# Later due times for side steps of a two-layer hybrid kernel: scan units split in three, and norm, filter, turn and gate steps placed behind more projections

## The chip, the cores and the metric

The kernel runs on one core of one Trainium2 chip, in one launch. The metric is the device time of an execution in microseconds (us). The same kernel varies from run to run by about 0.2%, so two medians that differ by less than that are not told apart.

## The reference

Two layers work on 128 context tokens and 512 latent tokens of width 1024. Each layer has a token mixer of three branches and then a SwiGLU FFN; both have a norm, a modulation and a gated residual. Cut to what the change touches:

```python
def trunk_layer(x, mod, s0, p):
    sh1, sc1, g1, sh2, sc2, g2 = jnp.split(mod, 6, axis=-1)
    h = rmsnorm(x, p['norm1_g']) * (1.0 + sc1) + sh1
    y, s_fin = parallel_mixer(h, s0, p)
    x = x + g1 * y
    h = rmsnorm(x, p['norm2_g']) * (1.0 + sc2) + sh2
    x = x + g2 * swiglu(h, p['w_gu'], p['w_down'])
...
def delta_mixer(qkv_raw, z, b_raw, a_raw, conv_w, a_log, dt_bias, norm_w, s0):
    qkv = jax.nn.silu(centred_dwconv(qkv_raw, conv_w).astype(f32))
    q = l2norm(qkv[..., :H_A * DK].reshape(bn, L, H_A, DK)) * (DK ** -0.5)
    k = l2norm(qkv[..., H_A * DK:2 * H_A * DK].reshape(bn, L, H_A, DK))
    beta = jax.nn.sigmoid(b_raw.astype(f32))
    g = -jnp.exp(a_log.astype(f32)) * jax.nn.softplus(a_raw.astype(f32) + dt_bias.astype(f32))
    # forward and backward gated_delta_chunked(q, k, v, g, beta, s0)
...
def gated_delta_chunked(q, k, v, g, beta, s0):      # chunks of 64 tokens
    decay = jnp.exp(jnp.where(incl, gc[..., :, None] - gc[..., None, :], -jnp.inf))
    a_low = jnp.where(strict, jnp.einsum('bhnid,bhnjd->bhnij', kb, k) * decay, 0.0)
    m = a_low + jnp.eye(CHUNK, dtype=a_low.dtype)
    u = triangular_solve(m, v * beta[..., None])     # and w; then a scan over chunks
...
def hyena_filters(L, w1, b1, freq, w2, b2, w3):
    h = jnp.sin(fq * (zpos @ w1.astype(f32) + b1.astype(f32)))
    h = jnp.sin(fq * (h @ w2.astype(f32) + b2.astype(f32)))
    h = h @ w3.astype(f32)                           # then a window, and an FFT over tokens
```

## The kernel before

All 640 tokens are worked on together as two halves of 320 columns (`c` = 0, 1), channels on partitions. A projection is a sum of products of 128x128 weights with 128x320 activations. Each fp32 product is made of three matmuls of split operands (`wh`, `wl` are the upper and lower part of a weight tile). Three such matmuls, `pg<-A,wh` twice and `pg<-A,wl` once, are called a *triple* below.

The order of the instructions on all engines is fixed when the program is written out, and it is a planner that fixes it. There is a main stream, the projections of a layer in turn (q, k, v; FNet input; z; Hyena input; gates; output; FFN). Beside it run *side* coroutines, which hold the work that isn't a projection: `filters` (the Hyena filter network and its transform), `delta_gates`, `delta_qk` (normalises q and k and turns them), `delta_v`, the three batches of the chunked scan (`prep` with `delta_unit` and `delta_inv`, and `scan` with `delta_step`), `mods`, `fnet`, `hyena`, and `rstd` (the two halves of a norm's reciprocal root). After every two triples the main stream calls `pump`, which may let a side do its next step, up to its next `yield`. It does so when the time at which the step's inputs will be ready, as a crude cost model has it (`co.t`), is not later than the modelled time of TensorE:

```python
for co in sorted(self.sides, key=lambda co: co.t):
    ...
    if not co.done and self.ready(co) and co.t <= c["pe"] + co.hint:
        self.step(co)
```

So a number added to `cur.t` inside a side puts its next step further back among the projections. Where the main stream needs a side's result, it calls `finish`, and the steps that are left are written out in a row with no projection between them. There are three such places in a layer that matter here. One is behind the v projections of layer 1, `self.finish(self.ff, self.gm)`, where the rest of the filter network must be done. The next is ahead of the gates:

```python
while self.dst() is None:
    self.finish_one(gd)
```

`dst` is the end of batch 1, the four forward latent chunks of the scan. The third is the end of a norm, whose normalised tiles the next projections need.

A scan unit (`delta_unit`, 10 for a layer, four to a batch and two in batch 0) is a chunk pair in one direction. Before, its first step has three GpSimd passes of 128x512: two that make the right sides `rhs` from the gate sums `dgh` (written as `U<-dgh,small`), and one that makes mask times beta (`small,dsel`). The next step has the two matmuls `ps<-U,stcr` on the right sides, an exponential on ScalarE, and a GpSimd product. `stagger` runs two units side by side. `delta_inv` then inverts the 64x64 systems (matmuls `A,A 32x32` are its first stage), and `delta_step` runs the scan (`S,A` are its products with the state).

Every operation goes through one helper line, L2189, so all instructions of the trace have that line; they are told apart by tiles. `T`, `U`, `A` are pools of work tiles of 640, 512 and 2560 columns, `ps` and `pg` are tiles of PSUM, `rb` the broadcast reciprocal root. `stcr`, `par`, `small` are constants, `dgh`, `dsel`, `dex` results of `delta_gates`, `dsr` and `dss` of the rsqrt in `delta_qk`.

Of the kernel before, what the change touches and what calls it, by code (L numbers as in the profile page):

```python
# [303 lines left out]
class _Net:  # L304
# [472 lines left out]
    def rstd(self, u, n, w):  # L777

        nc = self.nc
        if u == 0:  # L780
            self.rb = []
        self.on(self.ssq[:, u:u + n * w])
        yield 0.0
        ps = self.ps()
        for t in range(n):
            nc.tensor.matmul(ps[:w, t:t + 1], self.ssq[:, u + t * w:u + t * w + w], self.ones[:, 0:1],
                             start=True, stop=True)
        m = self.p2.tile([P, 5], F32, tag="nm", name=self.nm("nm"))[:w, :n]
        r = self.p2.tile([P, 5], F32, tag="nr", name=self.nm("nr"))[:w, :n]
        nc.vector.tensor_scalar(out=m, in0=ps[:w, :n], scalar1=1.0 / D, scalar2=EPS, op0=ALU.mult, op1=ALU.add)  # L790
        self.rsqrt(r, m)
        dg = (self.U() if u or n * w < T else self.Tt())[:w, :n * w]
        nc.vector.tensor_tensor(out=dg.rearrange("p (t j) -> p t j", t=n),
                                in0=self.ident[:w, None, :w].to_broadcast([w, n, w]),
                                in1=r[:, :, None].to_broadcast([w, n, w]), op=ALU.mult)
        yield 0.0
        for c in range(n * w // NC):
            ps = self.ps()
            nc.tensor.matmul(ps[:, :NC], self.ones[:w], dg[:, c * NC:(c + 1) * NC], start=True, stop=True)
            self.rb.append(ps[:, :NC])  # L800
# [117 lines left out]
    def filters(self, l):  # L918
# [30 lines left out]
        for sl in (slice(0, TS), slice(TS, T)):  # L949
            n = sl.stop - sl.start  # L950
            ps = self.ps()
            nc.tensor.matmul(ps[:64, :n], mw[:33, 0:64], zp[:33, sl], start=True, stop=True)
            self.sin_mlp(ps[:64, :n], 64, fq[:64], bb[:64, 0:1], h1[:64, sl], n)
            yield
            ps = self.ps()
            nc.tensor.matmul(ps[:, :n], mw[:64, 64:192], h1[:64, sl], start=True, stop=True)
            h2 = self.U()
            self.sin_mlp(ps[:, :n], P, fq, bb[:, 1:2], h2[:, :n], n)
            nc.scalar.copy(hs[:64, sl], h2[:64, :n])
            th = self.U(F32R)  # L960
            nc.scalar.copy(th[64:, :n], h2[64:, :n])
            nc.vector.tensor_tensor(out=hs[64:, sl], in0=h2[64:, :n], in1=th[64:, :n].bitcast(F32), op=ALU.subtract)
            yield
        if not l:
            self.pre = True
# [144 lines left out]
    def delta_qk(self):  # L1110

        nc = self.nc
        self.kt = self.A()
        kt = self.kt.rearrange("p (t c) -> p t c", t=5)
        q, k = self.q, self.k
        def one(t):
            cols = slice(t * P, (t + 1) * P)
            ss = self.p2.tile([P, 16], F32, tag="dss", name=self.nm("dss"), bufs=3)
            qn = self.U()
            for n, (src, dst) in enumerate(((q, qn), (k, kt[:, t]))):  # L1120
                ps = self.ps()
                for m in range(4):
                    nc.tensor.transpose(ps[:, m * P:(m + 1) * P], src[:, m, cols], self.ident)
                sq = self.U()
                nc.scalar.activation(sq, ps, AF.Square)
                nc.scalar.copy(dst, ps)
                nc.vector.tensor_reduce(out=ss[:, n * 8:n * 8 + 8], in_=sq.rearrange("p (h d) -> p h d", d=64),
                                        axis=AX.X, op=ALU.add)
            yield
            r = self.p2.tile([P, 16], F32, tag="dsr", name=self.nm("dsr"), bufs=3)  # L1130
            nc.vector.tensor_scalar(out=ss, in0=ss, scalar1=EPS, scalar2=None, op0=ALU.add)
            self.rsqrt(r, ss)
            nc.vector.tensor_scalar(out=r[:, 0:8], in0=r[:, 0:8], scalar1=0.125, scalar2=None, op0=ALU.mult)
            for n, dst in enumerate((qn, kt[:, t])):
                dv = dst.rearrange("p (h d) -> p h d", d=64)
                nc.vector.tensor_tensor(out=dv, in0=dv, in1=r[:, n * 8:n * 8 + 8, None].to_broadcast([P, 8, 64]),
                                        op=ALU.mult)
            yield
            for src, dst in ((qn, q), (kt[:, t], k)):
                ps = self.ps()  # L1140
                for m in range(4):
                    nc.tensor.transpose(ps[:, m * P:(m + 1) * P], src[:, m * P:(m + 1) * P], self.ident)
                nc.scalar.copy(dst[:, :, cols], ps.rearrange("p (m t) -> p m t", m=4))

        yield from self.stagger([one(t) for t in range(5)], 3)

    def delta_v(self):
# [12 lines left out]
    def delta_gates(self, l, ba):  # L1160
# [2 lines left out]
        nc = self.nc  # L1163
        v = nc.vector
        ab = self.par[l][1]
        ps = self.ps()
        for t in range(5):
            nc.tensor.transpose(ps[:, t * 32:(t + 1) * 32], ba[:32, t * P:(t + 1) * P], self.ident[:32, :32])
# [62 lines left out]
    def delta_unit(self, N, Pm, u, s, t):  # L1231

        nc = self.nc
        rhs = []
        mk = self.mask[:, s]
        for n in range(2):
            r = self.U(F32R)
            nc.gpsimd.tensor_tensor(out=r.rearrange("p (c i) -> p c i", i=64),
                                    in0=self.ghl[:, n, s, t, :, None].bitcast(F32).to_broadcast([P, 8, 64]),
                                    in1=mk[:, None, :].to_broadcast([P, 8, 64]), op=ALU.mult)  # L1240
            rhs.append(r)
        E, mb = N[:, u], Pm[u]
        nc.gpsimd.tensor_tensor(out=mb, in0=mk[:, None, :].to_broadcast([P, 8, 64]),
                                in1=self.beta[:, s, t].rearrange("p b a -> p (b a)")[:, :, None].to_broadcast([P, 8, 64]),
                                op=ALU.mult)
        yield
        ps = self.ps()
        nc.tensor.matmul(ps, self.stcr[:, s], rhs[0], start=True, stop=False)
        nc.tensor.matmul(ps, self.stcr[:, s], rhs[1], start=False, stop=True)
        nc.scalar.activation(E, ps.rearrange("p (c i) -> p c i", i=64), AF.Exp)  # L1250
        nc.gpsimd.tensor_tensor(out=E, in0=E, in1=mb, op=ALU.mult)
        yield
        pk = [self.ps(), self.ps()]
        for hh in range(4):
            for n, src in enumerate((self.k, self.q)):
                for h2, par in DIAG:
                    pr = slice(64 * h2, 64 * h2 + 64)
                    c0 = t * P + par * 64
                    nc.tensor.matmul(pk[h2][64 * par:64 * par + 64, hh * P + n * 64:hh * P + n * 64 + 64],
                                     self.k[pr, hh, c0:c0 + 64], src[pr, hh, c0:c0 + 64], start=True, stop=True)  # L1260
        for h2 in range(2):
            pv = pk[h2].rearrange("p (c n i) -> p c n i", c=4, n=2)
            for dst, n in ((Pm[u], 1), (N[:, u], 0)):
                nc.vector.tensor_tensor(out=dst[:, h2 * 4:h2 * 4 + 4], in0=pv[:, :, n], in1=E[:, h2 * 4:h2 * 4 + 4],
                                        op=ALU.mult)
        yield
# [392 lines left out]
    def hyena(self, l):  # L1659
# [3 lines left out]
        for hf in range(2):  # L1663
# [4 lines left out]
            nc.sync.dma_start(z[:, :, 0:TP], src[:, :, 0:TP])  # L1668
            nc.sync.dma_start(z[:, :, TP:T], src[:, :, TP + 1:T + 1])
            self.on(S)  # L1670
            yield
            for o in range(2):
                zs = z[:, :, TP:T]
# [566 lines left out]
```

## Time and profile before

| | us |
|---|---|
| runs | 2749.70, 2753.47, 2746.98 (median 2749.7) |
| profiled execution | 2748.93, of which the span of the trace is 2747.2 |
| TensorE (PE) busy | 2542.1 (93%) |
| VectorE (DVE) busy | 1784.8 (65%) |
| GpSimd (POOL) busy | 1272.3 (46%) |
| ScalarE (ACT) busy | 1101.5 (40%) |

TensorE's mean granted clock over the span was 0.963 of full speed. "Idle" in the text is time in which TensorE runs no matmul; the profile names the instruction that ended each such wait.

### The profile page before, as it was taken

What the parts mean: (1) busy time and instruction counts of PE and PEld (TensorE: products, weight loads), DVE (VectorE), ACT (ScalarE), POOL (GpSimd) and SP (SyncE); (2) the same over time, 40 slices, a digit from 0 to 9 for tenths busy, and PEclk for the clock granted to TensorE, in tenths of its full rate; (3) what the DMA queues carried; (4) which work ended last, traced back from release to release, by engine and by line L of the source; (5) the groups of instructions that cost most, each with busy time, mean ns of one, the idle gap of its engine ahead of it and who ended that gap; (6) DMA issues with size and microseconds to landing.
All of it is one profiled execution on the core that took longest, in us unless ns stands there. A gap on an engine that the chain in (4) does not pass through costs nothing. (4 is left out here: it accounts for less than half of the span.)

```text
span 2747.2 us, 55957 instructions
## 1 busy us (share of the span) xinstructions
PE 2542.1 (93%) x22520; PEld 2411.4 (88%) x22520; DVE 1784.8 (65%) x3375; ACT 1101.5 (40%) x2383; POOL 1272.3 (46%) x1228
## 2 busy tenths in 40 slices
PE   5897999979999999999988989889999999999998
PEld 3786988979999999999977779778889998999997
DVE  5467977444645686667665789665456358777775
ACT  4454464422332343333335544534223333444442
POOL 2334325332335576666632352333333365776662
PEclk8998999989999999999989999989999999999999
DMA  7442663534554235422222437425255441222222
GB/s 295 171 164 63 162 146 90 155 134 146 204 191 169 62 128 173 162 78 85 85 97 90 144 79 184 115 65 159 95 200 193 163 167 47 85 85 77 85 76 79
DMA packets 125683, 353.57 MB, mean 129 GB/s; under 512 B 11994, under 2 KB 26330, under 8 KB 118944
## 3 DMA queue, kind: packets, MB, share of 16 engines
q1 hardware_dynamic: 107856, 312.76, 34.2%
q0 software_dynamic: 17568, 37.24, 7.1%
q8 instruction: 177, 2.90, 0.4%
q14 instruction: 82, 0.67, 0.1%
HBM read 288.60 MB, written 37.24 MB: 119 GB/s over the span
## 5 line engine op out<-in xcount | busy, mean ns | idle before, releaser
L2189 PE MATMUL pg<-A,wh 128*128 128x320 f32 (+1 forms) x6304 | 1456.0, 318 | 44.3 <-POOL A L2189 10.4
L2189 PEld LDWEIGHTS pg<-A,wh 128*128 128x128 f32 (+1 forms) x6304 | 1070.5, 192 | 87.0 <-POOL A L2189 18.0
L2189 PE MATMUL pg<-A,wl 128*128 128x320 f32 (+1 forms) x3152 | 990.5, 314 | 2.3 <-DMA wl<-wr 1.8
L2189 POOL TENSOR_TENSOR wl<-wr,wh 128x512 fp32r<-128x512 f32 (+2 forms) x374 | 524.3, 1415 | 513.8 <-ACT wh L2189 486.4
L2189 PEld LDWEIGHTS pg<-A,wl 128*128 128x128 f32 (+1 forms) x3152 | 603.5, 191 | 7.1 <-DMA wl<-wr 4.2
L2189 ACT CAST wh<-wr 128x512 fp32r<-128x512 f32 (+2 forms) x486 | 287.0, 609 | 278.8 <-PE pg L2189 231.4
L2189 PE MATMUL ps<-A,wh 128*128 128x320 f32 x1696 | 378.8, 310 | 0.0
L2189 PEld LDWEIGHTS ps<-A,wh 128*128 128x128 f32 x1696 | 283.9, 188 | 1.4 <-issue 1.0
L2189 PE MATMUL ps<-A,wl 128*128 128x320 f32 x848 | 263.5, 311 | 5.0 <-POOL wl L2189 4.8
L2189 POOL TENSOR_TENSOR wl<-U,wh 128x512 fp32r<-128x512 f32 x160 | 227.8, 1441 | 43.5 <-ACT wh L2189 43.5
L2189 POOL DMA_DIRECT2D wl<-wr x112 | 98.7, 912 | 277.7 <-ACT wl L2189 264.6
L2189 PE MATMUL ps<-A,A 32*32 32x32 f32 (+5 forms) x2984 | 205.3, 239 | 9.3 <-DVE A L2189 5.5
L2189 PEld LDWEIGHTS ps<-A,A 32*32 32x32 f32 (+2 forms) x2984 | 177.3, 142 | 20.2 <-DVE A L2189 6.0
L2189 DVE TENSOR_TENSOR T<-T,T 128x320 f32<-128x320 f32 (+1 forms) x139 | 133.6, 961 | 83.7 <-ACT T L2189 79.4
L2189 POOL TENSOR_TENSOR A<-A,A 128x640 fp32r<-128x640 f32 (+5 forms) x84 | 122.2, 1473 | 121.0 <-ACT A L2189 113.1
L2189 DVE TENSOR_TENSOR A<-A 128x120 f32<-128x120 f32 (+23 forms) x690 | 161.0, 297 | 14.0 <-DMA A<-hyS 10.8
L2189 PEld LDWEIGHTS ps<-A,wl 128*128 128x128 f32 x848 | 159.7, 188 | 7.4 <-POOL wl L2189 7.3
L2189 ACT CAST wh<-U 128x512 fp32r<-128x512 f32 x160 | 99.2, 621 | 165.4 <-PE ps L2189 60.0
L2189 PE MATMUL pg<-A,A 128*128 128x320 f32 x1056 | 161.0, 310 | 0.0
L2189 PEld LDWEIGHTS pg<-A,A 128*128 128x128 f32 x1056 | 156.3, 188 | 0.7 <-issue 0.2
L2189 DVE STREAM_TRANSPOSE A<-A 32x1024 f32<-32x1024 f32 x72 | 151.2, 2120 | 1.5
L2189 DVE TENSOR_TENSOR U<-ps,U 128x512 f32<-128x512 f32 x144 | 77.9, 542 | 103.3 <-PE ps L2189 66.8
(165 smaller groups left out, 3194.7 us busy)
## 6 DMA issues: line engine op xcount, KB each, us to landing
wr<-in_wbig_dram SPq DMA_DIRECT2D x272, 512.0 KB, 3.7
A<-in_wmod_dram SPq DMA_DIRECT2D x40, 1024.0 KB, 6.4
A<-hT SPq DMA_DIRECT2D x32, 1024.0 KB, 7.7
wl<-wr POOLq DMA_DIRECT2D x112, 256.0 KB, 4.5
kSp<-U SPq DMA_DIRECT2D x40, 256.0 KB, 2.0
U<-kSp SPq DMA_DIRECT2D x40, 256.0 KB, 8.7
A<-in_wmod_dram SPq DMA_DIRECT2D x16, 512.0 KB, 10.2
hyS<-T SPq DMA_DIRECT2D x24, 320.5 KB, 3.1
```

The costliest lines, as they stand in the source:

```text
L2189: return f(*a, **k)
```

## The change

No instruction changes its operands. Numbers are added to the due times of some steps, and three `yield` lines are new: one at the start of `delta_gates`, with a wait on its input, and one behind each of the two `rhs` passes of `delta_unit`, so that the unit's three GpSimd passes stand in three steps.

```diff
     def rstd(self, u, n, w):            # u > 0: second half of a norm
         self.on(self.ssq[:, u:u + n * w])
+        if u:
+            self.cur.t += 3.0
         yield 0.0
...
+        if u:
+            self.cur.t += 3.0
         yield 0.0
         for c in range(n * w // NC):
...
     def filters(self, l):               # after the first, and after the second sin step
+            if l:
+                self.cur.t += 3.0
             yield
...
     def delta_qk(self):
+            self.cur.t += 2.0
             yield
             for src, dst in ((qn, q), (kt[:, t], k)):
...
     def delta_gates(self, l, ba):
         ab = self.par[l][1]
+        self.on(ba[:32])
+        self.cur.t += 2.5
+        yield
         ps = self.ps()
...
     def delta_unit(self, N, Pm, u, s, t):
             rhs.append(r)
+            self.cur.t += 1.5
+            yield
         E, mb = N[:, u], Pm[u]
...
     def hyena(self, l):
             self.on(S)
+            self.cur.t += 1.5
             yield
```

What this does to the order is seen best on TensorE, at three places.

The first is in layer 0, the two units of batch 0 (`U,stcr`) among the k and v projections. Before:

```order
L2189 MATMUL pg_2317<-A_449,wl_2119 128x320
L2189 MATMUL ps_2345<-U_2329,stcr 128x512
L2189 MATMUL ps_2345<-U_2331,stcr 128x512
L2189 MATMUL ps_2350<-U_2334,stcr 128x512
L2189 MATMUL ps_2350<-U_2336,stcr 128x512
L2189 MATMUL pg_2317<-A_450,wh_2123 128x320
```

And in the changed kernel, where the units come behind the rest of that projection and behind the start of the next one (`pg_2366`):

```order
L2204 MATMUL pg_2317<-A_450,wl_2124 128x320
L2204 MATMUL ps_2360<-small,A_428 128x128 x4
L2204 MATMUL pg_2366<-A_449,wh_2118 128x320
L2204 MATMUL pg_2366<-A_451,wh_2118 128x320
L2204 MATMUL pg_2366<-A_449,wl_2119 128x320
L2204 MATMUL pg_2366<-A_449,wh_2118 128x320
L2204 MATMUL pg_2366<-A_451,wh_2118 128x320
L2204 MATMUL pg_2366<-A_449,wl_2119 128x320
L2204 MATMUL ps_2373<-U_2329,stcr 128x512
L2204 MATMUL ps_2373<-U_2339,stcr 128x512
L2204 MATMUL ps_2378<-U_2331,stcr 128x512
L2204 MATMUL ps_2378<-U_2341,stcr 128x512
```

The four matmuls have moved behind six more triples. On GpSimd the passes of the two units stood as two `rhs`, one mask, two `rhs`, one mask; now the four `rhs` come first and the two masks last, still six in a row.

The second place is in layer 1, where the filter network (`U,T` its taps, `A,A` its transform) runs beside the last q, k, v projections. Before, pieces of it alternate with pairs of triples up to the end of the projections:

```order
L2189 MATMUL ps_17196<-U_17050,T_16221 128x512
L2189 MATMUL ps_17196<-U_17051,T_16221 128x512
L2189 MATMUL pg_17203<-A_15731,wh_16951 128x320
L2189 MATMUL pg_17203<-A_15733,wh_16951 128x320
L2189 MATMUL pg_17203<-A_15731,wl_16952 128x320
L2189 MATMUL pg_17203<-A_15731,wh_16951 128x320
L2189 MATMUL pg_17203<-A_15733,wh_16951 128x320
L2189 MATMUL pg_17203<-A_15731,wl_16952 128x320
L2189 MATMUL ps_17210<-A_16687,A_16685 128x512
L2189 MATMUL ps_17210<-A_16688,A_16685 128x512
L2189 MATMUL ps_17210<-A_16687,A_16685 128x512
```

At the same rows of the changed kernel the projections have run out, and filter work follows filter work:

```order
L2204 MATMUL pg_17061<-A_15732,wh_16868 128x320
L2204 MATMUL pg_17061<-A_15734,wh_16868 128x320
L2204 MATMUL pg_17061<-A_15732,wl_16869 128x320
L2204 MATMUL ps_17133<-U_16962,T_16221 128x512
L2204 MATMUL ps_17133<-U_16963,T_16221 128x512
L2204 MATMUL ps_17145<-U_16962,T_16221 128x512
L2204 MATMUL ps_17145<-U_16963,T_16221 128x512
L2204 MATMUL ps_17152<-A_16806,A_16804 128x512
L2204 MATMUL ps_17152<-A_16807,A_16804 128x512
```

Behind the last q, k, v projection there stand 10 `U,T` and 48 `A,A` matmuls before, and 26 and 84 now; 28 triples have moved ahead of that filter work. The steps of the filter network ahead of it, its sines and first taps, stand 4 to 26 triples later.

The third place is the end of layer 1's Hyena projections, ahead of the loop on `dst`. Before, units of the last batch still have projections beside them:

```order
L2189 MATMUL ps_20100<-A_17945 64x64 x16
L2189 MATMUL ps_20119<-U_20027,stcr 128x512
L2189 MATMUL ps_20119<-U_20029,stcr 128x512
L2189 MATMUL pg_20018<-A_15732,wh_19617 128x320
L2189 MATMUL pg_20018<-A_15734,wh_19617 128x320
L2189 MATMUL pg_20018<-A_15732,wl_19618 128x320
```

Now the last projections stand ahead of the first forward step of the scan, and nothing of the main stream is left behind them:

```order
L2204 MATMUL pg_19753<-A_15732,wh_19559 128x320
L2204 MATMUL pg_19753<-A_15734,wh_19559 128x320
L2204 MATMUL pg_19753<-A_15732,wl_19560 128x320
L2204 MATMUL ps_19882<-A_17804 64x64 x16
L2204 MATMUL ps_19906<-U_19899,U_19808 64x64
L2204 MATMUL ps_19907<-U_19899,U_19808 64x64 x2
```

Thirty triples that stood beside the scan have moved ahead of it. All four forward steps (`S,A`), the last 128 matmuls of the last batch's first inverse stage, and its units now lie behind the last projection; before, one step of four and the inverse stage lay ahead of it.

Elsewhere the moves are smaller, counted in triples on TensorE. The transposes of `delta_gates` move back by 8 (layer 0) and 12 (layer 1). The turns of `delta_qk` move by 2 to 4. The first products of a Hyena half move by 2 to 4. The second half of a norm moves too: the column sums (`small,T`) by 8, and then the broadcast (`U,small`), which stood 8 triples behind the sums of layer 1's FFN norm, stands behind 4 triples and 30 other matmuls of the same size. The broadcast of layer 1's first norm moves by 8 triples. The number of matmuls, and of instructions on VectorE and GpSimd, is the same.

## Rows read from the trace of the kernel before

**Rows 1.** Page: the span, and busy time, share and instructions of two engines

```profile
span 2747.2 us, 55957 instructions
PE 2542.1 (93%) x22520; PEld 2411.4 (88%) x22520; DVE 1784.8 (65%) x3375; ACT 1101.5 (40%) x2383; POOL 1272.3 (46%) x1228
```

**Rows 2.** Waits of TensorE: whom for, us in total, times, longest

```profile
PE ps L2189 <- POOL U L2189: 8.7, 11, 2.1
```

**Rows 3.** Timeline of TensorE, layer 0: start, us, operation [idle before, releaser]

```profile
94.28 0.61 PE L2189 MATMUL ps<-small,T 32*128 32x32 f32 x5 [2.30 <-DVE T L2189]
...
126.51 1.51 PE L2189 MATMUL ps<-U,T 128*128 128x512 f32 x2 [4.70 <-ACT U L2189]
...
211.96 0.63 PE L2189 MATMUL ps<-small,U 128*128 128x128 f32 x4 [3.25 <-DVE U L2189]
...
229.02 1.12 PE L2189 MATMUL ps<-small,A 128*128 128x128 f32 x4 [5.13 <-ACT A L2189]
...
243.95 0.50 PE L2189 MATMUL ps<-U,stcr 128*128 128x512 f32 x1 [2.13 <-POOL U L2189]
```

**Rows 4.** Timeline of TensorE, layer 1 up to q, k, v

```profile
1446.89 0.49 PE L2189 MATMUL ps<-small,T 32*128 32x32 f32 x5 [2.31 <-DVE T L2189]
...
1483.18 0.48 PE L2189 MATMUL ps<-T,U 64*128 64x128 f32 x2 [3.87 <-ACT T L2189]
...
1501.25 0.50 PE L2189 MATMUL ps<-U,T 128*128 128x512 f32 x1 [1.44 <-ACT U L2189]
...
1582.52 0.92 PE L2189 MATMUL ps<-small,U 128*128 128x128 f32 x4 [2.97 <-DVE U L2189]
```

**Rows 5.** Stretches: us, busy PE, PEld, DVE, ACT, POOL; PEclk, DMA share, GB/s

```profile
94.30:100.00 5.70, 5.70 (x51) 4.54 (x52) 2.56 (x8) 2.98 (x8) 0.00 (x0) 0.70 1.05 368
...
243.90:254.00 10.10, 8.16 (x62) 6.56 (x66) 6.55 (x2) 3.39 (x7) 5.41 (x6) 0.66 0.19 56
...
1447.00:1452.00 5.00, 5.00 (x23) 3.96 (x24) 2.21 (x7) 4.37 (x8) 0.00 (x0) 0.76 0.44 163
...
1483.20:1488.00 4.80, 4.35 (x19) 4.16 (x20) 2.02 (x2) 2.63 (x8) 2.66 (x6) 0.64 0.00 0
```

**Rows 6.** A stretch of layer 1's last q, k, v projections, columns as in rows 5

```profile
1526.00:1555.00 29.00, 29.00 (x148) 23.51 (x147) 19.03 (x27) 15.09 (x37) 10.26 (x17) 1.00 0.60 185
```

**Rows 7.** Layer 1, last q, k turn: TensorE, VectorE, GpSimd timelines

```profile
1602.64 1.09 PE L2189 MATMUL ps<-small,U 128*128 128x128 f32 x4 [6.41 <-DVE U L2189]
...
1594.57 0.18 DVE L2189 SCALAR_TENSOR_TENSOR rs<-rs,dss 128x16 f32<-128x16 f32 x1
1594.78 6.78 DVE L2189 SCALAR_TENSOR_TENSOR dsr<-rs,dsr 128x16 f32<-128x16 f32 x1
...
1595.18 2.37 POOL L2189 TENSOR_TENSOR U<-dgh,small 128x512 fp32r<-128x512 f32 x2
...
1600.19 1.33 POOL L2189 TENSOR_TENSOR U<-small,dsel 128x512 f32<-128x512 f32 x1
```

**Rows 8.** Layer 1, scan: TensorE timeline, and stretches as in rows 5

```profile
1756.05 3.12 PE L2189 MATMUL ps<-A,A 32*32 32x32 f32 x126 [3.93 <-DVE A L2189]
...
1788.49 1.97 PE L2189 MATMUL ps<-A 64*64 64x64 f32 x32 [8.06 <-DVE A L2189]
...
1640.00:1680.00 40.00, 36.20 (x233) 35.41 (x232) 38.92 (x126) 15.78 (x33) 16.34 (x27) 0.96 0.71 159
...
1752.00:1798.00 46.00, 33.81 (x688) 30.93 (x690) 19.02 (x17) 20.98 (x53) 16.89 (x26) 0.81 0.31 78
1798.00:1832.00 34.00, 23.24 (x791) 20.75 (x785) 19.28 (x38) 11.73 (x35) 19.05 (x19) 0.80 0.18 43
```

**Rows 9.** Norms: TensorE timeline, and a stretch as in rows 5

```profile
1416.05 1.43 PE L2189 MATMUL ps<-U,small 80*128 80x320 f32 x2 [1.83 <-DVE U L2189]
...
2290.88 0.73 PE L2189 MATMUL ps<-small,T 128*80 128x1 f32 x8 [3.17 <-DVE T L2189]
...
2310.00:2320.00 10.00, 10.00 (x70) 10.00 (x69) 9.96 (x7) 2.20 (x4) 10.00 (x6) 1.00 0.18 49
```

More of the change, by code (lines that the diff above doesn't have):

```diff
@@ L962, in filters @@
             nc.vector.tensor_tensor(out=hs[64:, sl], in0=h2[64:, :n], in1=th[64:, :n].bitcast(F32), op=ALU.subtract)
+            if l:
+                self.cur.t += 3.0
             yield
```

## The prediction

> **What bounds the kernel now.** I read the page first. TensorE is busy for 2542.1 of 2747.2 us, 93%, and the next engine, VectorE, for 65% [rows 1]. So TensorE sets the time, and what a new order can win is TensorE's idle time, 2747.2 - 2542.1 = 205 us, and what comes behind it. I then read TensorE's waits by releaser: the list is long and flat, and one of its entries, a wait for GpSimd's work tiles, comes to 8.7 us in 11 waits [rows 2]. Next I read TensorE's timeline for each wait that ends at an instruction which the change moves [rows 3, 4], and last the stretches right behind such waits. There the reader is to see the granted clock: it is 0.70, 0.66, 0.76 and 0.64 in the 5 to 10 us behind four waits of 2 to 4 us [rows 5], between the two levels of 1.2 and 2.4 GHz. So a wait costs more than its idle time. By these rows the extra loss is (1 - clock) times the length: 1.7, 3.4, 1.2 and 1.7 us. These are estimates from the rows, since the work of those stretches isn't all matmul.
>
> One limit holds in layer 1 that doesn't in layer 0. VectorE is near its own bound there: 38.92 of 40 us are busy in a stretch of the scan, and just behind it TensorE waits for VectorE in a row of waits that ends at 1832 [rows 8].
>
> **The change part by part.** It adds and removes no work on TensorE. It puts more triples ahead of a side's matmuls, so each term is a wait that triples now fill, less what is missing where these triples stood. At full clock 10.00 us hold 70 such matmuls [rows 9], so a triple is 0.43 us.
>
> *Gates.* `delta_gates` comes 8 and 12 triples later, 3.4 and 5.1 us. Its waits of 2.30 and 2.31 us [rows 3, 4] are covered by that, and the slow clock behind them, 1.7 and 1.2 us [rows 5], goes with them. Sum 7.5. Late next is the unit that needs the gate sums, which is itself moved. I take all of it; the lower end is 4.6, the idle time alone.
>
> *Filter network of layer 1.* A sin step waits 3.87 us for ScalarE, a tap behind it 1.44 [rows 4], and the clock behind the first costs 1.7 [rows 5]: 7.0. All of it is filled, since these steps move back by 4 to 26 triples. But 28 triples, 28 x 0.43 = 12.0 us, stood among the filter's transform in the 29 us from 1526 to 1555. Without them TensorE has 29.0 - 12.0 = 17.0 us of work there and VectorE 19.03 [rows 6]. So that stretch becomes VectorE's, and at least 19.0 - 17.0 = 2 us come back as waits. I take 3, since a chain without cover also waits for each hand-over, and so 4 net. The ends are 1.5 (a third of 17 us idle, as in the uncovered scan [rows 8]) and 7.
>
> *Turns of q, k.* In layer 0 the waits of 3.25 and 5.13 us [rows 3] get 2 to 4 triples, 0.9 to 1.7 us, each: with the clock behind the longer one, some 1.7 as behind the gates, 4 in all. In layer 1 the 2.97 us wait [rows 4] gets 4 triples. I take 1.5. The 6.41 us wait [rows 7] gets two, and its cause is another. A VectorE instruction of 128x16, of which the one before it took 0.18 us, took 6.78 us, just while GpSimd ran six 128x512 passes without a gap from 1595.18 to 1601.5 [rows 7]. They are the scan units' passes. In the changed program these six still stand next to each other on GpSimd, so I leave that wait where it is. Sum 5.5, ends 2 and 10.
>
> The Trainium skill ("SBUF — State Buffer", section "Who interferes with whom") says that a VectorE instruction with two SBUF inputs and a GpSimd instruction that reads SBUF lock each other out for one whole instruction. By it the held instruction loses one pass, 1.33 us, and the sum would win 5 us more wherever the passes come apart. By the row the hold lasts as long as the train, and the sum stays. The measured 6.78 us decides: the trace disagrees with one pass.
>
> *Scan units.* In layer 0 the `U,stcr` matmuls wait 2.13 us for GpSimd's right sides, and all such waits come to 8.7 us [rows 2, 3]. They stand 6 to 12 triples later now, 2.6 us or more at full clock, which is longer than the longest wait. I take 6 of the 8.7, and 2 of the 3.4 us of clock behind the first [rows 5]: 8, ends 4 and 12.
>
> *Taps in layer 0.* The 4.70 us wait at 126.51 [rows 3] has ScalarE queued behind VectorE's convolution. The gates' exponentials, which share that queue, move off. It may shrink or stay: 0, ends 0 and 4.7.
>
> *Hyena halves* get 2 to 4 triples, which are missing a little later: 0, ends -1.7 and +1.7 (four triples).
>
> *Norms.* The column sums of layer 1's FFN norm wait 3.17 us [rows 9], and eight triples now stand ahead. But the broadcast stands 4 triples and 30 matmuls behind the sums, 42 x 0.143 = 6.0 us, where 8 triples took 3.4. After it VectorE normalises, and is already full: 9.96 of 10 us [rows 9]. VectorE's chain starts 1 to 2.6 us later, and TensorE follows it. Layer 0 has the same pattern. For layer 1's first norm the wait of 1.83 us [rows 9] goes, and the broadcast is 3.4 - 1.8 = 1.6 us later. I take -2 for the three, ends -5 and +8.
>
> *End of layer 1's scan.* TensorE idles (46.0 - 33.8) + (34.0 - 23.2) = 23 us from 1752 to 1832 [rows 8]. Thirty triples, 12.9 us, now stand ahead of that. They cover the waits of 3.93 and 8.06 us [rows 8] if the chain behind these isn't later itself. Against this the fourth forward step is now without cover, and the last batch's inverse and units too. Uncovered, a third of the time is idle (10.8 of 34 [rows 8]), about 3.2 us for each step of some 10. Best: 12 - 3.2 = +9. Worst: the chain stays and all the cover is lost, -12.9 - 3.2 - 8.1 (the held VectorE instruction once more) = -24.2. I take -3, because VectorE is nearly full through this scan.
>
> The sum: 7.5 + 4 + 5.5 + 8 + 0 + 0 - 2 - 3 = 20 us. The profiled execution took 2748.9 (its span and 1.7 around it) and so comes to 2728.9; the median of the runs is 0.8 above it. **Forecast 2730 us**; its own range is 2718 to 2742.
>
> **The rivals.**
>
> *Layer 1 gives its part back.* If VectorE, not TensorE, carries layer 1 up to the end of the scan, what gates (2.31 + 1.2), filter (4) and turns (1.5) win there becomes waiting at the loop on `dst`: 2730 + 9 = 2739. For it: VectorE's 38.92 of 40 us. Against it: TensorE was still busy for 36.20 of these 40 [rows 8].
>
> *The GpSimd trains break up.* If the passes, now steps of their own, come with gaps, the held VectorE instructions cost one pass each instead of a train. The waits of 6.41 and 8.06 us fall to 1.33 us each, by 5.1 and 6.7: 2718. For it: that is where the trains lie. Against it: in batch 0 the six passes stay neighbours.
>
> *Slower: the end of layer 1's scan stays VectorE's chain.* Then the cover is lost as priced (-24.2 in place of -3) and the layer 1 gains don't count (9): 2730 + 21.2 + 9 = 2760. For it: 80 us with 23 idle today, all behind that one chain. Against it: the 3.93 and 8.06 us waits are just what more triples ahead would fill. It decides from a loss of 19 us at that place: 2730 + 9 + 16 = 2755.
>
> *Nothing comes of it.* Each filled wait comes back a few steps later as another, in both layers, since the inputs that the sides wait for aren't earlier: about 2749. For it: the list of waits is flat, with no large entry to take away. Against it: in layer 0 TensorE runs without long waits behind the moved places.
>
> **How the numbers follow.** Forecast 0.45, layer 1 gives back 0.20, trains break 0.10, slower scan 0.13, nothing 0.12. A difference under 0.2%, 5.5 us, can't be told from none by runs that vary this much. Faster than 2744.2: 0.45 + 0.10 + 0.17 of the 0.20, 0.72. Within: the 0.12 and 0.03 of the 0.20, 0.15. Slower than 2755.2: 0.13. The 8-in-10 range takes in the broken trains and "nothing", and leaves out the slower scan: 2710 to 2755. Below 2710 lie only sums in which several terms reach their upper ends.
>
> **What would show it.** Right: in the changed trace no wait over 0.5 us at `small,T 32x32` in either layer; GpSimd's entry among TensorE's waits under 3 us; no wait near 4 us in layer 1's sin steps, and a stretch of some 40 us of uncovered filter work with 3 to 5 us idle; a 6 to 7 us hold of a small VectorE instruction still there in layer 1's turn; column sums without a wait but TensorE waiting for VectorE's normalised tiles 1 to 2 us more. The forecast is wrong if the idle time from layer 1's last Hyena projection to its gates is over 40 us (slower scan), or if the held instruction falls to under 2 us (trains broken), or if layer 0 reaches its gates less than 10 us earlier than now.

## The result: slower by 1.0%, and the profile after

The changed kernel takes 2776.76 us (median of 4 runs, 2772.12 to 2783.73) against 2748.55 (4 runs): a ratio of 1.0102, with a 95% interval of 1.0076 to 1.0127. The forecast was 2730. Its profiled execution took 2772.12 us, so it lies at the fast end of its runs.

The page of the changed kernel, to be held against [rows 1]:

```profile
span 2770.0 us, 55928 instructions
PE 2554.5 (92%) x22520; PEld 2420.7 (87%) x22520; DVE 1792.4 (65%) x3375; ACT 1102.7 (40%) x2382; POOL 1270.0 (46%) x1228
```

TensorE's idle time is 215.5 us (205 before), and its busy time grew by 12.4 us with no matmul added: the mean granted clock is 0.956, 0.963 before. The view of TensorE's waits, against [rows 2]:

```profile
PE ps L2204 <- DVE A L2204: 31.5, 29, 5.8
PE ps L2204 <- ACT U L2204: 28.0, 12, 7.2
PE ps L2204 <- POOL U L2204: 19.3, 3, 8.9
```

The wait for GpSimd that was to vanish has more than doubled, in 3 waits in place of 11. TensorE's timeline shows where, and what became of [rows 3, 4, 7]:

```profile
130.51 2.93 PE L2204 MATMUL ps<-A,A 128*128 128x512 f32 x6 [7.16 <-ACT U L2204]
...
230.20 1.12 PE L2204 MATMUL ps<-small,A 128*128 128x128 f32 x4 [5.24 <-ACT A L2204]
...
251.07 0.47 PE L2204 MATMUL ps<-small,A 128*128 128x128 f32 x1 [7.24 <-ACT A L2204]
...
287.06 0.80 PE L2204 MATMUL ps<-U,stcr 128*128 128x512 f32 x1 [8.89 <-POOL U L2204]
...
1546.99 0.80 PE L2204 MATMUL ps<-U,T 128*128 128x512 f32 x1 [4.42 <-ACT U L2204]
...
1608.19 0.63 PE L2204 MATMUL ps<-small,U 128*128 128x128 f32 x4 [1.80 <-DVE U L2204]
1649.75 0.79 PE L2204 MATMUL ps<-U,stcr 128*128 128x512 f32 x1 [8.93 <-POOL U L2204]
```

Some waits that the forecast named are gone (2.30 and 2.31 at the gates, 3.87 at the sin step), and the 6.41 us at the turn are 1.80. Others stayed or grew: the 5.13 us at `small,A` in layer 0 are 5.24, a later group of the same form now waits 7.24, and the 4.70 us for ScalarE at the taps are 7.16 at the transform behind them. In place of the sin step's wait, two projections of layer 1 wait 3.40 and 2.98 us for ScalarE. The new wait of 8.9 us comes in both layers at the same instruction: the second right side of a unit. GpSimd's timeline in layer 0 says why:

```profile
273.60 1.67 POOL L2204 TENSOR_TENSOR U<-dgh,small 128x512 fp32r<-128x512 f32 x1
284.87 1.16 POOL L2204 MEMSET A<- 128x1024 f32 x2 [9.60 <-DVE A L2204]
285.96 2.05 POOL L2204 TENSOR_TENSOR U<-dgh,small 128x512 fp32r<-128x512 f32 x2
```

and VectorE's, what the memset waits for:

```profile
282.00 1.68 DVE L2204 TENSOR_TENSOR A<-ps,A 128x256 f32<-128x256 f32 x4
283.60 1.22 DVE L2204 TENSOR_TENSOR A<-A 128x1024 f32<-128x1024 f32 x1
286.07 4.38 DVE L2204 TENSOR_TENSOR A<-A 128x31 f32<-128x31 f32 x4 [1.26 <-POOL A L2204]
```

`delta_inv` of batch 0 clears half of its work tile a second time, on GpSimd, after a VectorE addition that ends at 284.82. The new `yield` between a unit's two passes let the planner write that memset pair between them. GpSimd works in order, so the second pass, which needs nothing from VectorE, waited behind it, and TensorE behind the pass. In layer 1 the same pair waits 9.84 us, up to 1647.56.

The other large losses show in stretches of the changed kernel, against [rows 6, 8]. The columns are us, busy PE, PEld, DVE, ACT, POOL; PEclk:

```profile
1540.00:1560.00 20.00, 15.07 (x42) 9.31 (x41) 12.56 (x17) 6.85 (x15) 4.92 (x5) 0.74 0.52 167
1560.00:1580.00 20.00, 17.95 (x64) 12.46 (x63) 13.48 (x18) 7.70 (x14) 5.89 (x5) 0.91 0.21 79
1752.00:1790.00 38.00, 32.40 (x435) 29.97 (x435) 19.18 (x42) 21.97 (x60) 11.34 (x28) 0.91 0.61 147
1790.00:1818.00 28.00, 18.05 (x497) 16.24 (x496) 13.02 (x15) 12.22 (x29) 10.69 (x12) 0.58 0.24 61
1818.00:1847.00 29.00, 21.73 (x772) 19.61 (x771) 14.36 (x35) 9.86 (x30) 18.86 (x19) 0.87 0.01 3
```

In the first two, filter work without projections, TensorE idles 7.0 us and loses 0.26 x 20 + 0.09 x 20 = 7.0 more to the clock. No engine is full there: VectorE is busy for 26 of 40 us and TensorE for 33. I read that as a chain in which each step waits for the one before it. In the last two, the scan's end, it idles 17.2 us at a clock of 0.58 and 0.87. From 1752 up to the gates the loss (idle and clock) is 5.6 + 3.4 + 17.2 + 15.5 = 41.7 us, and by [rows 8] it was 12.2 + 8.7 + 10.8 + 6.8 = 38.5 before. The waits that the thirty triples filled came back behind them.

All projection matmuls run in the same order in every kernel here, so the traces can be laid side by side by the start of the same matmul. Us in each part (the rest ends at the last such matmul), and forward scan steps that lie without projections at the loop on `dst`, which I call bare steps:

| kernel (profiled run) | layer 0 | l1 q,k,v + filter | l1 FNet to gates | l1 next 480 | rest | steps l0, l1 |
|---|---|---|---|---|---|---|
| before | 1398.5 | 173.0 | 260.9 | 104.3 | 795.1 | 0, 3 |
| changed | 1398.3 | 181.3 | 267.1 | 111.1 | 796.7 | 0, 4 |
| memset_on_vector | 1388.5 | 181.5 | 265.5 | 114.2 | 804.6 | 0, 4 |
| no_units | 1408.9 | 181.6 | 260.0 | 106.0 | 798.9 | 0, 3 |
| units_alone | 1431.8 | 172.2 | 255.8 | 106.3 | 793.4 | 3, 1 |
| pair_in_one_step | 1441.0 | 181.5 | 264.4 | 113.6 | 797.2 | 2, 4 |
| filters_alone | 1395.6 | 180.3 | 260.6 | 104.3 | 795.5 | 0, 3 |
| gates_alone | 1395.8 | 178.7 | 261.9 | 104.4 | 795.2 | 0, 3 |
| gates_layer0 | 1399.9 | 172.0 | 263.1 | 104.4 | 798.7 | 0, 3 |
| filters_earlier | 1403.1 | 172.6 | 261.4 | 106.0 | 793.5 | 0, 3 |
| units_layer1 | 1397.8 | 172.9 | 257.5 | 106.3 | 793.3 | 0, 1 |
| units_layer1_vec | 1394.9 | 172.9 | 251.0 | 106.2 | 799.6 | 0, 1 |
| units_layer1_turns | 1401.3 | 172.1 | 263.6 | 110.7 | 798.5 | 0, 4 |
| layer0_turns_units | 1387.7 | 173.0 | 250.6 | 106.2 | 799.9 | 0, 1 |
| layer0_gates_units | 1427.4 | 173.2 | 250.9 | 106.3 | 799.6 | 3, 1 |

Parts that are coded alike differ by up to 7.5 us between single profiled runs: layer 0 is that of the kernel before in filters_alone (1395.6) and in filters_earlier (1403.1), and the rest is alike in units_layer1 (793.3) and gates_layer0 (798.7). Idle time is about the same in these (101.5 and 100.5 us; 35.4 and 35.5); the granted clock makes the difference. The changed kernel's 22.8 us of span are 8.3 in layer 1's filter, 6.2 + 6.8 in its scan, and 1.6 behind it, most of it at the FFN norm. Layer 0 reaches its gates at 465.97, 1.2 us earlier than before, is 5.4 us ahead at its 2100th projection matmul, behind its scan (585.6, and 591.0 before), and gives that back by layer 1's start.

### The profile page after: what moved, and what is told of

Same layout as the page of the kernel before. It is cut to its first block, busy times and chain, and to the rows that moved or that the text cites. A ratio compares the mean times of both kernels' runs of the same rounds, so it can differ in the third digit from the quotient of the medians.

```text
span 2770.0 us, 55928 instructions
## 1 busy us (share of the span) xinstructions
PE 2554.5 (92%) x22520; PEld 2420.7 (87%) x22520; DVE 1792.4 (65%) x3375; ACT 1102.7 (40%) x2382; POOL 1270.0 (46%) x1228
## 5 line engine op out<-in xcount | busy, mean ns | idle before, releaser
L2204 PE MATMUL ps<-A,A 32*32 32x32 f32 (+5 forms) x2984 | 212.2, 244 | 18.3 <-DVE A L2204 8.3
L2204 PEld LDWEIGHTS ps<-A,A 32*32 32x32 f32 (+2 forms) x2984 | 183.3, 146 | 31.6 <-DVE A L2204 7.5
L2204 DVE TENSOR_TENSOR A<-A 128x120 f32<-128x120 f32 (+23 forms) x690 | 173.0, 316 | 9.7 <-DMA A<-hyS 4.5
L2204 DVE SCALAR_TENSOR_TENSOR T<-T,par,T 128x641 f32<-128x641 f32 x84 | 107.4, 1279 | 74.8 <-POOL T L2204 34.1
```

The costliest lines, as they stand in the source:

```text
L2204: return f(*a, **k)
```

## The experiments

Edits are against the kernel before, unless another is named; ratios are to the kernel before, with 95% intervals.

**GpSimd's queue.** The changed kernel with

```diff
-            nc.gpsimd.memset(S[:, 1024:2048], 0.0)
-            nc.gpsimd.memset(S[:, 1024:2048][:, 0:1024:33], 1.0)
+            for sl, x in ((S[:, 1024:2048], 0.0), (S[:, 1024:2048][:, 0:1024:33], 1.0)):
+                self.tick("pool", "memset", sl, [])     # the planner's clocks as before
+                v._e.memset(sl, x)                      # but on VectorE
```

> The changed kernel, with one pair of memsets for each layer (the second clearing of the inverse's work tile, in batch 0) issued on VectorE and not on GpSimd; the order on TensorE and of everything else is that of the changed kernel. Theory A (GpSimd's queue): in the changed kernel this pair waits for VectorE and stands between the two right-side passes of a batch 1 unit, so TensorE waits 8.89 us at 287 and 8.93 us at 1650 for the second pass. With the pair on VectorE both waits go, and with some 2 us of slow clock behind each the time falls by 18 to 22 us, to 2755 to 2759. Theory B (the later order itself: filter work and scan of layer 1 without cover): the two waits only move to the next step of the same chain, and the time stays above 2770.

2770.29 us, 1.0076 (1.0061 to 1.0091). GpSimd's timeline of this kernel:

```profile
270.66 3.66 POOL L2205 TENSOR_TENSOR U<-dgh,small 128x512 fp32r<-128x512 f32 x3
273.68 1.64 POOL L2205 TENSOR_TENSOR A<-small,dsel 128x512 f32<-128x512 f32 x1
```

The passes run through and both 8.9 us waits are gone, so the cause of the waits is shown. But by the medians only 6.5 us come back, not 18 to 22, and the two intervals (this one and 1.0076 to 1.0127) overlap, so what the waits cost in all isn't told apart from nothing. Layer 0 gains 9.8 by the table, and in the profiled run layer 1 gives it back, most of it behind its scan. There the idle time is the same (36.3 us, and 35.9 in the changed kernel); the clock takes 22.9 us in place of 14.9. From FNet to gates, where the wait of 8.93 us stood, layer 1 gains only 1.6.

**Without the units' part**, the changed kernel less

```diff
-            self.cur.t += 1.5
-            yield
```

> The changed kernel without its part in the scan units (three passes in one step, as before); all other parts stay. Theory A: the memset pair stands behind all units' passes again, the two 8.9 us waits go, the 8.7 us of short waits for right sides come back in part: 2756 to 2764. Theory B: most of the loss is in the other parts, and the time stays at 2768 or above.

2769.76 us, 1.0070 (1.0054 to 1.0085). Theory B, then: the other five parts make 20.5 us of loss. In layer 1's scan, from FNet through the next 480 matmuls, only 0.8 us of the 13.0 are left (366.0 us in sum, 365.2 before), with three bare steps as before: the loss there came with the units' part.

**The units' part alone**, those two lines added to the kernel before.

> The kernel before with the part in the scan units alone. Theory A: here the memset pair stands behind three right sides, ahead of one mask and the last right side; TensorE waits for the last right side, less long than in the changed kernel or just as long, twice: slower than before by 8 to 22 us, 2757 to 2771. Theory B: the units' part is harmless, within 5 us of before or faster by up to 8.

2776.80 us, 1.0099 (1.0085 to 1.0113). As slow as the whole change, but elsewhere: layer 0 loses 33 us, and layer 1 is faster from FNet to gates although its memset wait is there. TensorE's two waits for a right side did come, as theory A has it (5.33 and 6.15 us), but the sum fitted neither theory. The order shows the difference: three forward steps without cover in layer 0 (none before), one in layer 1 (three before).

**A unit's right sides kept in one step**: the changed kernel with `if n:` ahead of that `yield`.

> The changed kernel with the yield between a unit's two right-side passes taken out, so that only the mask pass has a step of its own. The memset pair then stands behind both right sides of one unit of batch 1 and ahead of its mask and of the next unit. Theory A: one unit gets through, the next waits as long for its right sides, so the two long waits come back one unit later, somewhat shorter by the triples between: 2765 to 2777. If it is only the split pair that hurts, 2757. Theory B: as the changed kernel, 2772 to 2780, without a wait for right sides.

2813.17 us, 1.0222 (1.0198 to 1.0246), the slowest of all. The two long waits come back one unit later, as theory A has it (4.87 and 4.88 us), but the time is 36 us above its range. Two forward steps lie bare in layer 0, whose part takes 1441.0 us, and four in layer 1. In layer 0's bare stretch 8.7 us are idle and the clock takes 7.9; the other 26 of the 42.5 us that layer 0 loses lie outside it, the 4.87 us wait among them, and no run here takes them apart.

**Each small part alone**, with its lines of the diff:

```diff
+            if l:
+                self.cur.t += 3.0        # filters_alone, twice
...
+        if u:
+            self.cur.t += 3.0            # norms_alone, twice
...
+        self.on(ba[:32])
+        self.cur.t += 2.5
+        yield                            # gates_alone
...
+            self.cur.t += 2.0            # turns_alone
...
+            self.cur.t += 1.5            # hyena_alone
```

> The kernel before with the part in layer 1's filter network alone. 81 of its transform matmuls lie behind the last q, k, v projection, against 48 before and 84 in the changed kernel. As forecast: 4 us faster, ends 1.5 and 7, 2742 to 2748. As the changed kernel's trace suggests (7 us idle and 7 us of slow clock between 1540 and 1580, where before had 2 and none): slower by 5 to 10 us, 2754 to 2759, with waits of 3 to 4 us at the taps in the uncovered stretch.

2755.50 us, 1.0022 (1.0011 to 1.0032): the loss of 6 us as the second reading had it, and the filter's own part of the table is 7.3 us longer. Behind the last q, k, v projection 4.6 us are idle and the clock takes 3.4 (1.8 and none before); the longest wait at a tap is 1.98 us, less than expected.

> The kernel before with the part in the norms' second halves alone. As forecast: slower by 2 us, ends faster by 8 and slower by 5. By the changed kernel's trace, where each FFN norm costs some 2 us and layer 1's first norm wins little: slower by 2 to 5 us, 2751 to 2754.

2753.24 us, 1.0014 (1.0004 to 1.0025): 4 us slower. VectorE's timeline at layer 1's FFN norm:

```profile
2297.39 0.49 DVE L2193 TENSOR_TENSOR U<-small,nr 80x320 f32<-80x320 f32 x1
2297.80 0.48 DVE L2193 TENSOR_TENSOR T<-T,pg 128x320 f32<-128x320 f32 x1
2299.95 0.89 DVE L2193 TENSOR_TENSOR A<-A,ps 128x320 f32<-128x320 f32 x2 [1.68 <-PE ps L2193]
```

The same row in the kernel before:

```profile
2297.36 0.89 DVE L2189 TENSOR_TENSOR A<-A,ps 128x320 f32<-128x320 f32 x2 [2.08 <-PE ps L2189]
```

The normalising starts 2.6 us late, into a VectorE that has no slack [rows 9]. Up to the norm the two runs are within 0.5 us of each other.

> The kernel before with the new step and due time of delta_gates alone. As forecast: faster by 7.5 us, at least 4.6: 2742 to 2745. Rival: it also delays the filter network (69 transform matmuls behind the last projection, against 48), which gives back 4 to 6 us, so that 2745 to 2751 remain.

2755.83 us, 1.0025 (1.0013 to 1.0037). The rival's way, and more: no gain is left, since the filter's part of layer 1 takes 5.7 us longer.

> The gates' part in layer 0 alone. If the loss of gates_alone comes by layer 1's filter network: within 3 us of before. As forecast for one layer: 4 us faster. If later gates are a loss in themselves: half of the loss of gates_alone, some 3 us slower.

`if l == 0:` around the three lines of the gates. 2754.29 us, but the ratio of the two sets of runs is 1.0006 (0.9994 to 1.0018): no difference can be told, and the filter's part of layer 1 is back at 172.0. So the table puts the loss of later gates at the filter network behind them; the totals of the two kernels alone don't tell them apart. Filling layer 0's wait of 2.30 us won nothing: the steps behind it wait in its place, 1.56 us at a tap and 5.64 us for ScalarE at the transform, where the kernel before has the one wait of 4.70.

> The kernel before with the later due time of the q, k turns alone. As forecast: faster by 5.5 us, ends 2 and 10: 2739 to 2747. Rival: the turns wait for the same VectorE and ScalarE work as before, only a triple or two later, and the units behind them start later: within 3 us of before.

2752.96 us, 1.0009 (0.9999 to 1.0018): no gain, and a loss can't be told from none. Layer 0's waits at the turns were 3.25, 2.32 and 5.13 us and are 1.51, 3.21 and 5.13. The first has four triples more ahead of it (54 projection matmuls in a row, 42 before) and the second two fewer (18, and 24 before). Ahead of the third no projection stands, in either kernel: from 221.97 to 229.02 TensorE has only side work, and the wait ends with ScalarE.

> The part in Hyena's halves alone. As forecast: 0, ends 1.7 either way. The four other small parts measured 20.5 us in sum and the changed kernel without the units' part 20.5 too, so nothing should be left for this one: 2747 to 2752.

2756.35 us, 1.0027 (1.0016 to 1.0039): slower by 6 us, where I expected none. TensorE's, VectorE's and GpSimd's timelines in layer 0:

```profile
657.13 2.08 PE L2190 MATMUL ps<-small,A 128*128 128x128 f32 x10 [1.99 <-DVE A L2190]
...
654.83 0.49 DVE L2190 TENSOR_TENSOR A<-A,T 128x320 f32<-128x320 f32 x1
655.24 2.35 DVE L2190 TENSOR_TENSOR A<-A 128x512 f32<-128x512 f32 x2
...
654.91 1.53 POOL L2190 TENSOR_TENSOR wl<-wr,wh 128x512 fp32r<-128x512 f32 x1 [2.91 <-ACT wh L2190]
```

The VectorE pair in the kernel before:

```profile
652.07 1.29 DVE L2189 TENSOR_TENSOR A<-A 128x512 f32<-128x512 f32 x2
```

Four more triples stand ahead of `small,A`, and its wait grew from 0.92 to 1.99 us. Its input is made by the VectorE pair at 655.24, which belongs to the same delayed step, so the triples run ahead of the pair and can't cover it. The growth is the pair's first instruction, which took 1.75 us and 0.68 before, while GpSimd's pass of 654.91 ran. That is 1 us. From the 616 us to the 703 of the kernel before, by the same matmuls, this one idles 2.0 us more and the clock takes 3.4 more; most of what else layer 0 loses is clock, which differs as much between parts coded alike. So where all of the 6 us come from stays open.

> The opposite of filters_alone: 2.0 us taken off the due time of the two sin steps of layer 1's filter network in place of 3.0 added. 27 of its transform matmuls lie behind the last q, k, v projection, against 48 before and 81 in filters_alone. If cover at that end is what counts, faster than before, by up to 3 us, although TensorE waits longer at the sin steps; if the waits at the sin steps count, slower by 2 to 6.

The filter's two lines with `-= 2.0`. 2749.95 us, 1.0007 (0.9995 to 1.0019): no difference. Layer 1's sin steps lose some 8 us (its drift at the same matmuls goes from 4.8 to 12.9, and to 15.2 further on), and the end with more cover gives 11 back. A triple placed here is missing there.

**What the scan's end costs.** The units' part with `if self.lay == 1:`, and the memset pair on VectorE.

> The kernel before with the units' part in layer 1 alone, and the memset pair on VectorE. In layer 1 one forward step lies behind the last Hyena projection, against three before and four in the changed kernel; layer 0 is as before. Theory C (what counts is how many forward steps of the scan are left without projections beside them at the loop on dst, some 10 us each with their slow clock): two steps less, faster by 10 to 20 us, 2730 to 2740. Theory D (the units' later passes are a loss by themselves, wherever the steps lie): slower, 2752 or more.

2745.60 us, 0.9990 (0.9980 to 1.0000), at the edge of no difference. Direction as theory C, size not: in layer 1 9.9 us are won from FNet to the gates, and 6.4 given back behind them.

> As units_layer1_vec, but with the memset pair on GpSimd as in the kernel before. Theory A (GpSimd's queue): the pair holds up the units again in layer 1, one wait of some 9 us with slow clock behind it: 8 to 11 us slower than units_layer1_vec. If the scan behind it takes that up, as the changed kernel's end of scan did, no difference.

2747.57 us, 0.9994 (0.9984 to 1.0004). The wait is back (6.20 us at 1642.98). From FNet to the gates it costs 6.5 us, over the whole kernel 2, within what runs vary.

> units_layer1_vec plus the later turns of q, k. The turns alone cost 3.7 us. Here they also push the end of the scan of layer 1 over an edge: four forward steps, 128 matmuls of the last inverse stage and eight unit matmuls lie without cover in layer 1, against one step, none and four in units_layer1_vec. Theory C: slower than units_layer1_vec by 3 steps x 8 to 12 us, 24 to 36, plus the turns' own. Theory D: slower by 2 to 5, the turns' own.

2763.69 us, 1.0051 (1.0033 to 1.0069): 18 us slower than units_layer1_vec for two microseconds in a due time. FNet to gates takes 263.6 in place of 251.0. Theory C in kind; some 5 us a step, not 8 to 12, and some of that may be the inverse's, which lies bare too.

The units' part in both layers with the memset pair on VectorE, and in layer 0 alone the turns' line, or in its place the gates' three lines:

```diff
+            if self.lay == 0:
+                self.cur.t += 2.0        # layer0_turns_units, in delta_qk
...
+        if l == 0:
+            self.on(ba[:32])
+            self.cur.t += 2.5
+            yield                        # layer0_gates_units, in delta_gates
```

> The units' part in both layers, the turns' part in layer 0 alone, the memset pair on VectorE; norms, filters, gates and Hyena as before. No forward step of layer 0's scan and one of layer 1's lies behind the last projection. Theory C (uncovered forward steps decide): layer 0 wins some 8 to 12 us as it did in memset_on_vector up to its gates, layer 1 some 5 as in units_layer1_vec: 2731 to 2738, faster than both kernels. Theory D (later units are a loss by themselves): not faster than before.

> As layer0_turns_units, but in layer 0 the gates' part in place of the turns' part. The same passes, but three forward steps of layer 0's scan lie without cover. Theory C: slower than layer0_turns_units by 3 x 8 to 13 us: 2757 to 2775. Theory D: within 5 us of layer0_turns_units.

2736.39 us, 0.9953 (0.9938 to 0.9968), and 2773.23 us, 1.0081 (1.0066 to 1.0095). 37 us lie between two kernels that run the same passes and differ in which one of two small steps is late in layer 0. The stretch behind layer 0's last Hyena projection, first of layer0_gates_units, then of layer0_turns_units:

```profile
457.80:491.00 33.20, 21.88 (x743) 19.16 (x741) 21.63 (x36) 11.39 (x33) 18.20 (x19) 0.81 0.19 45
```

```profile
461.00:494.00 33.00, 33.00 (x228) 33.00 (x227) 32.31 (x118) 14.49 (x29) 8.12 (x10) 1.00 0.67 150
```

The one runs three scan steps bare, 11.3 us idle at a clock of 0.81; the other is at its gates already, full at full clock. The stretch ahead of it, from the same projection matmul to the last Hyena projection, in the same order:

```profile
396.20:457.80 61.60, 53.89 (x928) 49.56 (x928) 35.91 (x47) 31.15 (x78) 22.71 (x40) 0.86 0.46 119
```

```profile
406.30:461.00 54.70, 53.99 (x1222) 49.27 (x1221) 39.84 (x52) 30.05 (x82) 32.41 (x44) 1.00 0.37 90
```

The whole difference is layer 0's (1427.4 to 1387.7). By idle time and clock, the bare stretch shows 11.3 + 6.3 of it, some 6 us a step, and the stretch ahead 7.0 + 8.6 more than the other kernel's, so the chain is late before it is bare. Some 12 us stand behind the scan, 9 of them clock. And layer0_turns_units beats both kernels: it takes of the change the units' part and layer 0's turns, with the memset pair on VectorE, and nothing else.

## Why the prediction was wrong

**The step that failed** is the first of its sum: "each term is a wait that triples now fill, less what is missing where these triples stood". I priced what was filled with care and what was missing by guess. Both halves failed. What was missing: the triples are a fixed stock. Where a layer ends in side work without projections, as at the filter's end and at the loop on `dst`, a triple spent early is idle time later, and in a worse place: bare steps wait at their hand-overs, and the clock falls (0.58 from 1790 to 1818). What was filled: the inputs that the steps wait for aren't ready earlier, so in layer 0 the wait at the gates moved to the next steps (2.30 and 4.70 us became 1.56 and 5.64), and the three waits at the turns, 10.7 us in sum, are still 9.9. That is what the rival "nothing comes of it" said, and it stood at 0.12.

**Gates** (priced at 7.5 won): 6.6 lost alone, 5.7 of it at layer 1's filter network, which I took for a separate term. **Filters** (4 won): 6.2 lost. I priced the uncovered transform by VectorE's busy time, 3 us; in the changed kernel, where the gates delay it too, it has 7.0 idle and 7.0 of clock, and no engine is full in it. **Turns** (5.5 won): nothing won; the wait of 5.13, which I gave 2 to 4 triples, got none. **Hyena** (0): 6 lost, of which 1 us is a held VectorE instruction. A wait inside a step isn't covered by delaying the step. **Norms** (2 lost): 4 lost; the mechanism, VectorE's full chain starting up to 2.6 us later, was right.

**Scan units** (8 won): the short waits did go, but I did not ask what else could now be written between the passes, the memset that waits for VectorE. With it moved away the median is 6.5 us of the 28 lower, which isn't clear of noise. **End of layer 1's scan** (3 lost): 13.0 lost by the table (6.2 + 6.8). The memset's wait doesn't make it: without that wait the two columns come to 379.7 us, with it to 378.2. Without the units' part, and so with three bare steps, they come to 366.0.

Of the rivals, the slower one named one of the places, and 2760 was nearest to the result; but it stood at 0.13, and the loss of the other parts wasn't in it. Its sign was set too high: from layer 1's last Hyena projection to the gates 17 us are idle (10.6 before), not 40. The train of passes at layer 1's turn did not break up, as forecast, but the hold is gone all the same: the train of 1613 to 1619 now falls where VectorE has nothing to do. So the sign of a hold under 2 us came without its rival.

The small parts sum to 26.3 us by their medians, and together, as no_units, cost 20.5. They don't add: filters and gates each lengthen the filter's part (7.3 and 5.7), and together they lengthen it by 8.6. **Left open**: where Hyena's 6 us and most of pair_in_one_step's loss come from; and why the clock is lower behind the scan (the table's "rest") in the kernels with the memset on VectorE, where idle time is the same. Some of them lie hardly outside what parts coded alike differ by.

## What to carry to other kernels

Before moving work to cover a wait, ask first whether the input gets ready any earlier for the steps behind it; if not, the wait turns up there, as at layer 0's gates and turns. Then count the work that could cover it: a triple spent early is missing at the next join. So look at what is left uncovered at each join, and count its steps in the order. By the bare steps of both layers, kernels with one took 2736 to 2748 us, with three 2749 to 2770, with four 2764 to 2777, and the one with six 2813. That is an order, not a price: the loss of a step came out at some 5 to 13 us. And where a step is split, look in each in-order queue at what may now be written between its halves, and at what that waits for.

## What was unexpected of the hardware

The held VectorE instruction is a matter of timing alone: in the changed kernel none is held in layer 1 (6.78 us at the turn before, and 8.62 at 1779.39), and two are in layer 0. One took 7.43 us at 241.85 (7.40 before, at the same place), the other 8.66 (the first of this pair, and 0.89 when not held), while GpSimd runs eight passes from 408.93 to 417.25:

```profile
409.29 9.58 DVE L2204 SCALAR_TENSOR_TENSOR T<-T,par,T 128x641 f32<-128x641 f32 x2 [0.44 <-POOL T L2204]
```

The clock's share was larger than I had allowed: TensorE's busy time grew by 12.4 us with the same matmuls, more than half of the longer span.
